# Three softmaxes whose rows are turned by a product with a diagonal of inverse sums

## The chip, the cores and the metric

The kernel runs on one core of a Trainium2 chip. A core has a matrix engine (TensorE, PE in the profile, with its weight loads listed apart as PEld), three engines for elementwise work (VectorE or DVE, ScalarE or ACT, GpSimd or POOL) and a sync engine (SP) that issues most transfers. Matrix products land in PSUM, eight banks of 128 partitions by 512 float32 values; the other data live in SBUF or, between stages, in memory. The metric is the device time of one execution in microseconds (us).

## The reference: three blocks, each with attention in it

The program is a chain of three transformer-like blocks over 1024 tokens of 1024 features. Block one mixes gating, a state space branch and a cross attention of 4 heads to 256 memory rows. Block two mixes a gated recurrence, 6 heads of stick-breaking attention and 6 heads of forgetting attention, followed by a feed-forward part. Block three has a convolution branch and latent attention of 8 heads, again followed by a feed-forward part. Three of these attentions are softmaxes:

```python
# cross attention, block one
p = jax.nn.softmax(s * (XA_HEAD_DIM ** -0.5), axis=-1)
o = jnp.einsum('bhlm,bmhd->blhd', p, vh)
# forgetting attention, block two: causal, with a bias from cumulative gates
p = jax.nn.softmax(jnp.where(mask, s, NEG_BIG), axis=-1)
o = jnp.einsum('bhqs,bhsd->bhqd', p, v)
```

Latent attention in block three is a softmax over all 1024 keys. Stick-breaking attention is no softmax: its weights come from a running product of sigmoids, and nothing is divided by a sum.

## The kernel before

Activations lie with features on partitions and tokens along the free dimension, in two halves of 512 tokens. To keep float32 accuracy, most products are done in three parts (`mm3`, L286 to L290): each operand is split into a high and a low part of a type called F32R, and three of the four cross products are added in PSUM.

An attention head works as follows. For each block of 128 query tokens the scores go to a PSUM tile `sp` with tokens on partitions and keys along the row. DVE takes the negated maximum of each row (`mx`), ACT computes the exponentials into the SBUF tile `pp` and at the same time adds up each row into `den`, one number per partition. That is L995 to L998 in cross attention, L1672 to L1674 in `causal_head`, and L2176 to L2180 in `mla_head`.

Then the rows have to be turned, because the product with the values needs keys on partitions. For each slice of 128 keys, four 128x128 blocks of `pp`, one per block of query tokens, are transposed by PE into one bank `ps_t` (L1003, L1686, L2189; there are two such banks). `av` (L1011) copies the bank as a high part with ACT (L1020) and takes the low part with DVE (L1021); two products with the values add up in the bank `ps_o` (L1025, L1026). In stick-breaking heads, which share `causal_head`, L1023 and L1024 take the place of L1020 and L1021.

At the end of each half, `av_out` (L896) adds the two halves of partitions of `ps_o` into `yo` (L901, L902). For a softmax it also divides: it takes the reciprocal of each `den` (L906), spreads it to 128 columns and transposes it on PE into a bank `ps_t` (L907), so that the inverse sums lie along the free dimension, and multiplies `yo` by that (L908). The result goes to memory and is read back as input of the output product.

What sets the order of the work: a framework schedules all instructions at build time by their order in the program, their priorities and its own costs, and each engine then works through its list in that order. `staggered` (L1612) mixes two heads: scores of the first half of a head, then the turn and value product of the second half of the head before it, then the scores of the second half, then the turn of the first half. Between them, `pump` (L438) fetches pieces of side work, the output product of rows that are ready, at a lower priority.

Buffers matter as well. In `causal_head` the tiles `pp` of the first half (512 columns) have 5 buffers and those of the second half (1024 columns) have 6; one half of a head needs 4. In `mla_head` there are 8 for two halves. `L1647` fills two rows of a query tile on POOL at the start of each forgetting head.

Of the kernel before, what the change touches and what calls it, by code (L numbers as in the profile page):

```python
# [10 lines left out]
F32 = mybir.dt.float32  # L11
# [3 lines left out]
ALU = mybir.AluOpType  # L15
# [4 lines left out]
P = 128  # L20
# [3 lines left out]
HF = 512  # L24
# [151 lines left out]
class Kern:  # L176
# [716 lines left out]
                nc.sync.dma_start(ybd[64 * gb:64 * gb + 64, t, :].rearrange("(g c) k -> c g k", c=16), yo[t * 16:(t + 1) * 16])  # L893


    def av_out(self, po, odd, out, dens=None):  # L896

        nc = self.nc
        a, b = (64, 0) if odd else (0, 64)
        r = slice(a, a + 64)  # L900
        nc.scalar.copy(out[r, :], po[b:b + 64, :])  # L901
        nc.vector.tensor_tensor(out[r, :], po[r, :], out[r, :], op=ALU.add)  # L902
        if dens:
            tp = self.pt("t")
            for j, den in enumerate(dens):
                nc.vector.reciprocal(den, den)  # L906
                nc.tensor.transpose(tp[:, j * P:(j + 1) * P], den.to_broadcast([P, P]), self.ident)  # L907
            nc.vector.tensor_tensor(out[r, :], out[r, :], tp[r, :], op=ALU.mult)  # L908

    def v_stack(self, ps, vst, scale=1.0):  # L910

# [63 lines left out]
    def cross(self, pc, p1, xs, y, kst, vst):  # L975
        nc, d = self.nc, self.d
        for i in range(2):
            def ev(hf, ps):
                hi = pc.tile([P, HF], F32R, tag="qh", bufs=1, name="qh")
                lo = pc.tile([P, HF], F32R, tag="ql", bufs=1, name="ql")  # L980
                nc.scalar.mul(hi, ps, 0.125)
                nc.vector.scalar_tensor_tensor(lo, ps, 0.125, hi.bitcast(F32), op0=ALU.mult, op1=ALU.subtract)
                qs = [pc.tile([P, HF], F32R, tag="qs", bufs=2, name="qs") for _ in range(2)]
                self.stack_pair(hi, lo, qs)
                for o in range(2):
                    h = 2 * i + o
                    pp = pc.tile([P, 4, 256], F32, tag="pp", bufs=2, name="pp")
                    sp = self.pt("s", (P, 4, 256))
                    for tt in range(4):
                        for j in range(2):  # L990
                            nc.tensor.matmul(sp[:, tt, :], qs[o][:, tt * P:(tt + 1) * P], kst[h][:, j, :], start=j == 0, stop=j == 1)
                    if o == 0:
                        self.pump()
                    mx = self.small("mx", (P, 4))
                    nc.vector.tensor_reduce(mx, sp, axis=AX, op=ALU.max, negate=True)  # L995
                    den = self.small("den", (P, 4))
                    for tt in range(4):
                        nc.scalar.activation(pp[:, tt, :], sp[:, tt, :], AF.Exp, bias=mx[:, tt:tt + 1], accum_out=den[:, tt:tt + 1])  # L998
                    po = self.pt("o")
                    for m in range(2):  # L1000
                        tp = self.pt("t")
                        for tt in range(4):
                            nc.tensor.transpose(tp[:, tt * P:(tt + 1) * P], pp[:, tt, m * P:(m + 1) * P], self.ident)  # L1003
                        self.av(pc, tp, vst[m][:, h, :], po, m == 0, m == 1)
                    yo = p1.tile([P, HF], F32, tag="tmp", bufs=3, name="yo")
                    self.av_out(po, o, yo, [den[:, tt:tt + 1] for tt in range(4)])
                    r = slice(64 * o, 64 * o + 64)
                    nc.vector.scalar_tensor_tensor(y[6 + i][hf][r], yo[r], 0.5, y[6 + i][hf][r], op0=ALU.mult, op1=ALU.mult)
            self.gemm(d["w_in"][16 + i], xs, ev)
# [613 lines left out]
    def causal_head(self, pl, pa, src, h, yd, row, fox):  # L1623
        nc = self.nc
        qs = []
        for hf in range(2):
            q = self.h("qs", "S", F32R)
            nc.sync.dma_start(q.bitcast(F32), src["q"][h, :, hf * HF:(hf + 1) * HF])
            qs.append(q)
        kk, qa = [], qs  # L1630
        for j in range(2):
            k = pl.tile([P, T], F32R, tag="k", bufs=4, name="k")
            f = k.bitcast(F32)
            nc.sync.dma_start(f[0:64], src["k"][h, j])
            if fox is None or j == 0:
                nc.sync.dma_start(f[64:128], src["k"][h, j])
            else:
                nc.sync.dma_start(f[64:66], fox[h])
            kk.append(k)
        rows = P  # L1640
        if fox is not None:

            qa, rows = [], 66
            for hf in range(2):
                q = pl.tile([P, HF], F32R, tag="q2", bufs=2, name="q2")
                nc.sync.dma_start(q.bitcast(F32)[0:64], src["q"][h, 0:64, hf * HF:(hf + 1) * HF])
                nc.gpsimd.memset(q.bitcast(F32)[64:66], -1.0)  # L1647
                qa.append(q)
        odd = h % 2
        vst = pl.tile([P, KT, P], F32R, tag="vst", bufs=2, name="vst")  # L1650
        nc.sync.dma_start(vst.bitcast(F32), src["v"][:, :, h, :])
        parts = []
        for hf in range(2):
            pps, dens = [], []
            parts.append((pps, dens))
            for j in range(4 * hf, 4 * hf + 4):
                w = (j + 1) * P
                sp = self.pt("s", (P, T))
                for c0 in range(0, w, HF):
                    c = slice(c0, min(w, c0 + HF))  # L1660
                    t = slice((j % 4) * P, (j % 4 + 1) * P)
                    for i, (q, r) in enumerate(((qs[hf], P), (qa[hf], rows))):
                        nc.tensor.matmul(sp[:, c], q[:r, t], kk[i][:r, c], start=i == 0, stop=i == 1)
                        if i == 0 and c0 + HF >= w:
                            nc.tensor.matmul(sp[:, w - P:w], self.idb, self.strict if fox is None else self.cau, start=False, stop=False)
                pp = pa.tile([P, HF * (hf + 1)], F32, tag=f"pp{hf}", bufs=5 + hf, name="pp")
                if fox is None:
                    self.stick(sp, pp, w)
                else:
                    mx = self.small("fmx", (P, 1), bufs=12)  # L1670
                    den = self.small("fden", (P, 1), bufs=12)
                    nc.vector.tensor_reduce(mx, sp[:, :w], axis=AX, op=ALU.max, negate=True)  # L1672
                    self.last = nc.scalar.activation(pp[:, :w], sp[:, :w], AF.Exp, bias=mx, accum_out=den)
                    dens.append(den)  # L1674
                pps.append(pp)
                if j % 4 == 3:
                    self.pump()
            yield
        for hf, (pps, dens) in enumerate(parts):
            po = self.pt("o")  # L1680
            ns = 4 * hf + 4
            for s in range(ns):
                j0 = max(0, s - 4 * hf)
                tp = self.pt("t")
                for j in range(j0, 4):
                    nc.tensor.transpose(tp[:, j * P:(j + 1) * P], pps[j][:, s * P:(s + 1) * P], self.ident)  # L1686
                self.av(pa, tp, vst[:, s, :], po, s == 0, s == ns - 1, j0 * P, 1.0 if fox is None else None)
            yo = pa.tile([P, HF], F32, tag="yo", bufs=1, name="yo")
            self.av_out(po, odd, yo, dens)
            nc.sync.dma_start(yd[row + 64 * h:row + 64 * h + 64, hf * HF:(hf + 1) * HF], yo[64 * odd:64 * odd + 64])  # L1690
            yield

# [454 lines left out]
    def mla_head(self, pa, h, qd, kd, krd, vd, yd):  # L2147
        nc = self.nc
        odd = h % 2
# [15 lines left out]
        for hf in range(2):  # L2165
            pps, dens = [], []
            parts.append((pps, dens))
            for j in range(4):
                sp = self.pt("s", (P, T))
                t = slice(j * P, (j + 1) * P)  # L2170
# [6 lines left out]
                pp = pa.tile([P, T], F32, tag="pp", bufs=8, name="pp")  # L2177
                nc.scalar.activation(pp, sp, AF.Exp, bias=mx, accum_out=den)
                pps.append(pp)
                dens.append(den)  # L2180
                if j==3:
                    self.pump()
            yield
        for hf, (pps, dens) in enumerate(parts):
            po = self.pt("o")
            for s in range(KT):
                tp = self.pt("t")
                for j in range(4):
                    nc.tensor.transpose(tp[:, j * P:(j + 1) * P], pps[j][:, s * P:(s + 1) * P], self.ident)  # L2189
                self.av(pa, tp, vst[:, s, :], po, s == 0, s == KT - 1)  # L2190
            yo = pa.tile([P, HF], F32, tag="yo", bufs=1, name="yo")
            self.av_out(po, odd, yo, dens)
            nc.sync.dma_start(yd[512 + 64 * h:512 + 64 * h + 64, hf * HF:(hf + 1) * HF], yo[64 * odd:64 * odd + 64])
            yield

# [38 lines left out]
```

## Time and profile before

| | us |
|---|---|
| median of 3 runs | 3093.59 |
| lowest and highest | 3091.27, 3094.7 |
| the profiled execution | 3100.47 |
| its span | 3098.7 |
| PE busy in it | 3015.7 |
| DVE busy | 2298.5 |
| ACT busy | 1404.8 |
| POOL busy | 195.6 |

A row of the profile names the line, the engine and the operation, then output and inputs, then shape and count; after the bar come the busy time in us, the mean duration of one in ns, and the idle time of the engine just before such instructions with what ended it. `cn` is the tile of constants, in which the identity matrix lies. A row of the waits reads: who waited for whom, total us, times, longest. A row of a stretch gives from and to, then its length, then for each engine the busy time and the number of instructions, at last the granted clock of PE, the share of the DMA engines and GB/s. Matmul durations overlap, since a matmul starts before the end of the one ahead of it.

### The profile page before, as it was taken

What the parts mean: (1) busy time and instruction counts of PE and PEld (TensorE: products, weight loads), DVE (VectorE), ACT (ScalarE), POOL (GpSimd) and SP (SyncE); (2) the same over time, 40 slices, a digit from 0 to 9 for tenths busy, and PEclk for the clock granted to TensorE, in tenths of its full rate; (3) what the DMA queues carried; (4) which work ended last, traced back from release to release, by engine and by line L of the source; (5) the groups of instructions that cost most, each with busy time, mean ns of one, the idle gap of its engine ahead of it and who ended that gap; (6) DMA issues with size and microseconds to landing.
All of it is one profiled execution on the core that took longest, in us unless ns stands there. A gap on an engine that the chain in (4) does not pass through costs nothing.

```text
span 3098.7 us, 39672 instructions
## 1 busy us (share of the span) xinstructions
PE 3015.7 (97%) x14472; PEld 2452.9 (79%) x14472; DVE 2298.5 (74%) x3624; ACT 1404.8 (45%) x2215; POOL 195.6 (6%) x266
## 2 busy tenths in 40 slices
PE   8999999999989999999999999999999999999998
PEld 6787878777767777888888888877777888888877
DVE  7757784858589877777867646577779988888766
ACT  3254363424256664444434433255545544454453
POOL 0010012212100000000000022000000000000000
PEclk9999999999999999999999999999999999999999
DMA  4242433332474433444653346642132333365333
GB/s 150 64 119 62 129 126 112 86 85 70 139 195 137 120 126 138 150 150 170 246 199 110 129 114 188 189 145 67 45 121 85 106 102 105 107 222 172 106 99 102
DMA packets 210749, 394.01 MB, mean 127 GB/s; under 512 B 31637, under 2 KB 71957, under 8 KB 210426
## 3 DMA queue, kind: packets, MB, share of 16 engines
q1 hardware_dynamic: 210554, 391.47, 40.1%
q8 instruction: 114, 1.87, 0.2%
q14 instruction: 81, 0.66, 0.1%
HBM read 272.78 MB, written 114.87 MB: 125 GB/s over the span
## 4 chain that ended last, share of the span: by engine, by line
PE 47%; DVE 2%; DMA 2%; ACT 1%; issue 1%; SPq 0%; POOL 0%; POOLq 0%; DVEq 0%; ACTq 0%
PE ps_G L289 9%; PE ps_G L290 9%; PE ps_G L288 9%; PE ps_g L289 2%; PE ps_g L288 2%; PE ps_g L290 2%; PE ps_t L2189 2%; PE ps_o L1025 1%; PE ps_t L288 1%; PE ps_t L290 1%; PE ps_t L289 1%; PE ps_o L1026 1%; PE ps_s L288 1%; PE ps_s L289 1%; PE ps_s L290 1%
## 5 line engine op out<-in xcount | busy, mean ns | idle before, releaser
L288 PE MATMUL ps_G<-xsh,wh 128*128 128x512 f32 (+1 forms) x1024 | 398.8, 389 | 8.0 <-ACT xsh L469 6.1
L289 PE MATMUL ps_G<-xsl,wh 128*128 128x512 f32 (+1 forms) x1024 | 398.4, 389 | 1.5 <-DVE xsl L474 1.5
L290 PE MATMUL ps_G<-xsh,wl 128*128 128x512 f32 (+1 forms) x1024 | 397.9, 389 | 1.1 <-DVE wl L309 0.6
L282 ACT CAST wh<-wr 128x1024 fp32r<-128x1024 f32 (+1 forms) x151 | 154.3, 1024 | 272.9 <-PE ps_G L289 74.9
L283 DVE TENSOR_TENSOR wl<-wr,wh 128x1024 fp32r<-128x1024 f32 (+1 forms) x151 | 181.9, 1208 | 82.9 <-ACT wh L282 81.9
L288 PEld LDWEIGHTS ps_G<-xsh,wh 128*128 128x128 f32 x1024 | 193.6, 189 | 47.2 <-ACT xsh L469 6.1
L289 PEld LDWEIGHTS ps_G<-xsl,wh 128*128 128x128 f32 x1024 | 193.2, 189 | 40.6 <-DVE xsl L474 3.1
L290 PEld LDWEIGHTS ps_G<-xsh,wl 128*128 128x128 f32 x1024 | 193.2, 189 | 40.2 <-DVE wl L309 1.5
L288 PE MATMUL ps_g<-xsh,wh 128*128 128x512 f32 (+1 forms) x472 | 186.8, 396 | 0.3 <-ACT xsh L469 0.3
L289 PE MATMUL ps_g<-xsl,wh 128*128 128x512 f32 (+1 forms) x472 | 186.0, 394 | 0.4 <-DVE xsl L474 0.2
L290 PE MATMUL ps_g<-xsh,wl 128*128 128x512 f32 (+1 forms) x472 | 185.2, 392 | 0.0
L288 PE MATMUL ps_G<-xe,wh 128*128 128x512 f32 x440 | 173.2, 394 | 3.9 <-ACT xe L327 3.2
L289 PE MATMUL ps_G<-xe,wh 128*128 128x512 f32 x440 | 172.8, 393 | 0.2 <-DVE xe L328 0.2
L290 PE MATMUL ps_G<-xe,wl 128*128 128x512 f32 x440 | 172.5, 392 | 0.0
L1021 DVE TENSOR_TENSOR ptl<-ps_t,pth 128x512 fp32r<-128x512 f32 x216 | 132.4, 641 | 52.5 <-ACT pth L1020 51.1
L288 PE MATMUL ps_G<-wh,wph 128*128 128x512 f32 x432 | 168.2, 389 | 0.7 <-ACT fz L1325 0.7
L290 PE MATMUL ps_G<-wh,wpl 128*128 128x512 f32 x432 | 168.1, 389 | 0.0
L289 PE MATMUL ps_G<-wl,wph 128*128 128x512 f32 x432 | 168.1, 389 | 0.0
L1020 ACT CAST pth<-ps_t 128x512 fp32r<-128x512 f32 x216 | 112.1, 552 | 109.5 <-PE ps_t L2189 73.8
L308 ACT CAST wh<-hr 128x1024 fp32r<-128x1024 f32 (+1 forms) x98 | 99.8, 1018 | 64.2 <-PE ps_G L290 19.8
L308 ACT CAST wh<-ss 128x1024 fp32r<-128x1024 f32 x68 | 71.4, 1049 | 126.3 <-PE ps_G L289 83.7
L309 DVE TENSOR_TENSOR wl<-hr,wh 128x1024 fp32r<-128x1024 f32 (+1 forms) x98 | 115.6, 1183 | 16.9 <-ACT wh L308 16.9
(611 smaller groups left out, 7550.5 us busy)
## 6 DMA issues: line engine op xcount, KB each, us to landing
wr<-in_w_in_dram SPq DMA_DIRECT2D x65, 512.0 KB, 3.4
wr<-in_w_up_dram SPq DMA_DIRECT2D x44, 512.0 KB, 4.0
wr<-in_w_ff_dram SPq DMA_DIRECT2D x33, 512.0 KB, 4.0
hr<-hT SPq DMA_DIRECT2D x32, 512.0 KB, 3.6
r<-in_w_ff_dram SPq DMA_DIRECT2D x28, 512.0 KB, 4.8
h<-fa SPq DMA_DIRECT2D x48, 256.0 KB, 2.3
hT<-ft SPq DMA_DIRECT2D x48, 256.0 KB, 2.1
hr<-h SPq DMA_DIRECT2D x24, 512.0 KB, 3.8
```

What stands on the lines that cost most here:

```text
L282: nc.scalar.copy(hi[:, :n], raw[:, :n])
L283: nc.vector.tensor_tensor(lo[:, :n], raw[:, :n], hi[:, :n].bitcast(F32), op=ALU.subtract)
L288: mm(out, sh, mh, start=start, stop=False, **kw)
L289: mm(out, sh, ml, start=False, stop=False, **kw)
L290: mm(out, sl, mh, start=False, stop=stop, **kw)
L308: self.nc.scalar.copy(hi, src)
L309: self.nc.vector.tensor_tensor(lo, src, hi.bitcast(F32), op=ALU.subtract)
L1020: nc.scalar.copy(hi[:, c0:], tp[:, c0:])
L1021: nc.vector.tensor_tensor(lo[:, c0:], tp[:, c0:], hi[:, c0:].bitcast(F32), op=ALU.subtract)
L1025: nc.tensor.matmul(po[:, c0:], vs, hi[:, c0:], start=start, stop=False)
L1026: nc.tensor.matmul(po[:, c0:], vs, lo[:, c0:], start=False, stop=stop)
L2189: nc.tensor.transpose(tp[:, j * P:(j + 1) * P], pps[j][:, s * P:(s + 1) * P], self.ident)
```

## The change

Two helpers are new. `over` takes the reciprocal of a `den` and has POOL multiply the identity matrix by it, row by row, into a tile `dg`: a diagonal matrix of inverse sums. `turned` puts a block of `pp` into the bank. Without a diagonal it transposes as before. With one it is an ordinary product, `pp` block transposed times diagonal, of two float32 operands. What comes out is the transposed block, each column of which is multiplied by the inverse sum of its query token. So the turned rows are already normalized.

All three softmaxes use it: each gets four diagonals per half when its exponentials are made. The division at the end of `av_out` is gone (L903 to L908). Stick-breaking heads keep their transposes. The diagonals have 8 buffers in cross attention and 12 in the other two. In `causal_head` the buffers of `pp` go from 5 to 4 and from 6 to 5, for stick-breaking heads as well, as they share the code and the pool.

```diff
-    def av_out(self, po, odd, out, dens=None):
+    def av_out(self, po, odd, out):
...
-        if dens:
-            tp = self.pt("t")
-            for j, den in enumerate(dens):
-                nc.vector.reciprocal(den, den)
-                nc.tensor.transpose(tp[:, j * P:(j + 1) * P], den.to_broadcast([P, P]), self.ident)
-            nc.vector.tensor_tensor(out[r, :], out[r, :], tp[r, :], op=ALU.mult)
+
+    def over(self, pool, den, bufs):
+        g = pool.tile([P, P], F32, tag="dg", bufs=bufs, name="dg")
+        self.nc.vector.reciprocal(den, den)
+        self.nc.gpsimd.tensor_scalar(g, self.ident, den, None, op0=ALU.mult)
+        return g
+
+    def turned(self, out, x, by):
+        if by is None:
+            self.nc.tensor.transpose(out, x, self.ident)
+        else:
+            self.nc.tensor.matmul(out, x, by, start=True, stop=True)
...
+                    dg = [self.over(pc, den[:, tt:tt + 1], 8) for tt in range(4)]
...
-                            nc.tensor.transpose(tp[:, tt * P:(tt + 1) * P], pp[:, tt, m * P:(m + 1) * P], self.ident)
+                            self.turned(tp[:, tt * P:(tt + 1) * P], pp[:, tt, m * P:(m + 1) * P], dg[tt])
...
-                    self.av_out(po, o, yo, [den[:, tt:tt + 1] for tt in range(4)])
+                    self.av_out(po, o, yo)
...
-                pp = pa.tile([P, HF * (hf + 1)], F32, tag=f"pp{hf}", bufs=5 + hf, name="pp")
+                pp = pa.tile([P, HF * (hf + 1)], F32, tag=f"pp{hf}", bufs=4 + hf, name="pp")
...
-                    dens.append(den)
+                    dens.append(self.over(pa, den, 12))
...
-                    nc.tensor.transpose(tp[:, j * P:(j + 1) * P], pps[j][:, s * P:(s + 1) * P], self.ident)
+                    self.turned(tp[:, j * P:(j + 1) * P], pps[j][:, s * P:(s + 1) * P], dens[j] if dens else None)
...
-            self.av_out(po, odd, yo, dens)
+            self.av_out(po, odd, yo)
...
-                dens.append(den)
+                dens.append(self.over(pa, den, 12))
...
-                    nc.tensor.transpose(tp[:, j * P:(j + 1) * P], pps[j][:, s * P:(s + 1) * P], self.ident)
+                    self.turned(tp[:, j * P:(j + 1) * P], pps[j][:, s * P:(s + 1) * P], dens[j])
...
-            self.av_out(po, odd, yo, dens)
+            self.av_out(po, odd, yo)
```

## The prediction

> **What bounds the kernel now.** I read the page first (its shares and its chain), then the stages that the change touches, one row each, then the waits, the chain and the order of instructions inside one stage.
>
> ```profile
> span 3098.7 us, 39672 instructions
> PE 3015.7 (97%) x14472; PEld 2452.9 (79%) x14472; DVE 2298.5 (74%) x3624; ACT 1404.8 (45%) x2215; POOL 195.6 (6%) x266
> ```
> ```profile
> core 0: us, PE busy (x) PEld busy (x) DVE busy (x) ACT busy (x) POOL busy (x), PEclk, DMA share, GB/s
> 210.00:277.00 67.00, 66.87 (x355) 52.64 (x354) 46.78 (x94) 36.38 (x100) 6.17 (x4) 1.00 0.20 57
> 848.00:973.00 125.00, 108.53 (x587) 80.16 (x587) 111.38 (x143) 73.64 (x131) 0.00 (x0) 0.96 0.67 183
> 973.00:1112.00 139.00, 135.43 (x770) 103.40 (x769) 113.33 (x227) 90.50 (x204) 5.18 (x10) 1.00 0.35 102
> 2000.00:2280.00 280.00, 278.18 (x1430) 213.97 (x1429) 209.41 (x324) 163.18 (x290) 0.13 (x2) 1.00 0.29 88
> ```
>
> The four stretches are cross attention, the stick-breaking heads, the forgetting heads and latent attention. The first, third and fourth hold the three softmaxes that change. PE is busy for nearly all of them, at a granted clock of 1.00, while DVE is at 70 to 82% and POOL is almost empty. Since matmuls overlap, a busy PE is not yet a full PE. So I price by the distance from start to start.
>
> ```profile
> 2141.75 0.60 PE L2189 MATMUL ps_t<-cn,pp 128*128 128x128 f32 x4
> 2142.10 0.48 PE L290 MATMUL ps_g<-yth,wl 128*128 128x512 f32 x1
> 2142.59 0.50 PE L1025 MATMUL ps_o<-pth,vst 128*128 128x512 f32 x1
> 2142.92 0.40 PE L288 MATMUL ps_g<-yth,wh 128*128 128x512 f32 x1
> ...
> 2144.99 0.39 PE L289 MATMUL ps_s<-k,qs 96*128 96x512 f32 x1
> ...
> 2147.26 0.39 PE L290 MATMUL ps_s<-k,qs 96*128 96x512 f32 x1
> ```
>
> Ten steps of 512 columns from 2144.99 to 2147.26 take 2.27 us: 0.227 us each. Four transposes of 128 columns last 0.60 us, and one alone 0.27 (rows below), so three steps take 0.33: 0.110 us each. In latent attention 512 transposes and the 64 of L907 need 576 x 0.110 = 63.4 us, the other 854 matmuls 854 x 0.227 = 193.9: together 257 of 280 us, 92%. PE is the bound there, with about 23 us of holes. The holes are mostly as at 2142.10: L1025 starts 0.49 after its predecessor instead of 0.23, because ACT's copy of the turned rows (`pth`) was late. The waits say the same, for latent attention and then for the forgetting heads:
>
> ```profile
> PEld ps_o L1025 <- ACT pth L1020: 19.1, 70, 0.5
> ACT pp L2178 <- PE ps_t L2189: 6.8, 5, 1.4
> PEld ps_t L2189 <- DVE yo L908: 0.5, 2, 0.2
> ```
> ```profile
> PEld ps_o L1025 <- ACT pth L1020: 9.6, 32, 0.8
> PEld ps_t L1686 <- DVE yo L908: 1.4, 3, 0.5
> PE ps_o L1025 <- ACT pth L1020: 1.4, 5, 0.4
> POOL q L1647 <- PE ps_s L1663: 223.9, 9, 143.1
> ```
>
> The chain of waits between 2130 and 2165 us is on PE all the time:
>
> ```profile
> by line: PE ps_t L2189 20.4%; PE ps_o L1025 15.8%; PE ps_o L1026 11.4%; PE ps_s L289 10.5%; PE ps_s L290 10.5%; PE ps_s L288 10.5%; PE ps_g L290 6.7%; PE ps_g L289 6.0%; PE ps_g L288 6.0%; PE ps_t L907 2.5%; issue 0.0%
> ```
>
> **The change, part by part.** *The turn itself.* These are the instructions concerned, and one real float32 product of the same shape that the kernel already has, L888:
>
> ```profile
> L2189 PE MATMUL ps_t<-cn,pp 128*128 128x128 f32 x512 | 80.6, 272 | 0.1
> L1686 PE MATMUL ps_t<-cn,pp 128*128 128x128 f32 x432 | 71.4, 274 | 0.2
> L907 PE MATMUL ps_t<-cn,fden 128*128 128x128 f32 x112 | 18.7, 273 | 0.0
> L1003 PE MATMUL ps_t<-cn,pp 128*128 128x128 f32 x64 | 11.9, 277 | 0.0
> L888 PE MATMUL ps_t<-xg,tp 128*128 128x128 f32 x32 | 6.2, 275 | 0.0
> L907 PE MATMUL ps_t<-cn,den 128*128 128x128 f32 x32 | 6.1, 272 | 0.0
> ```
>
> A transpose is one record: 8 heads x 2 halves x 8 slices x 4 blocks = 512 at L2189. L1686 serves twelve heads of 36 blocks; only the six forgetting heads, 216 blocks, change. L1003 changes all 64. L888 stands in a loop of 4 groups inside 4 blocks, 16 products, and leaves 32 records: a product of two plain float32 operands is issued twice. What a pair costs shows where L888 and L889 alternate:
>
> ```profile
> 86.46 0.39 PE L889 MATMUL ps_t<-hs,wb 128*128 128x128 f32 x2
> ...
> 87.80 0.39 PE L889 MATMUL ps_t<-hs,wb 128*128 128x128 f32 x2
> ```
>
> There are five pairs between these two, so six steps in 1.34 us: 0.223 us a product, against 0.110 a transpose. Extra per product: 0.113 us.
>
> The Trainium skill (Perfetto Trace Analysis, section Transposes) says that a logical transpose should use the transpose operation and not a standard matmul, because transposes skip the arithmetic. The trace agrees: 0.110 against 0.223 us.
>
> 792 blocks change (512 + 216 + 64) and the 144 transposes of L907 go. Latent attention: 512 x 0.113 - 64 x 0.110 = +50.8 us. Forgetting heads: 216 x 0.113 - 48 x 0.110 = +19.1. Cross attention: 64 x 0.113 - 32 x 0.110 = +3.7. Together +73.6 us on the engine that bounds these stages.
>
> *What the holes give back.* In a pair of groups, PE issues eight transposes (0.88 us), one filler, and then waits for the copy of the first group. With products the second group alone takes 0.89 us, longer than that copy (0.55 us, below), so the wait could vanish. But the order of the instructions is laid out at build time, and the layout may pull L1025 forward and leave the same hole. Bounds: nothing, or all of 19.1 + 9.6 + 1.4 = 30.1 us. The layout decides, and no row shows how it will fall, so I take half: -15.1.
>
> ```profile
> L1020 ACT CAST pth<-ps_t 128x512 fp32r<-128x512 f32 x216 | 112.1, 552 | 109.5 <-PE ps_t L2189 73.8
> L908 DVE TENSOR_TENSOR yo<-yo,ps_t 64x512 f32<-64x512 f32 x36 | 24.6, 682 | 1.2
> L906 DVE RECIPROCAL fden<-fden 128x1 f32<-128x1 f32 x112 | 15.1, 154 | 19.8 <-ACT pp L2178 16.3 <-ACT pp L1673 3.4
> ```
>
> *The division at the end.* L908 leaves DVE: 24.6 us that lay under PE's work and are worth nothing there. What counts is PE's waits for it (0.5 + 1.4 = -1.9) and the one L908 that ends latent attention, where yo still goes to memory and back before the next product: -0.7.
>
> *The reciprocals* stay 144 in number and already run as soon as a sum is there (L906 above waits for ACT's exponentials). They cost nothing new on DVE, but now stand ahead of the turn.
>
> *The diagonals.* 144 tensor_scalar of 128x128 on POOL. The nearest rows:
>
> ```profile
> L622 POOL TENSOR_SCALAR ws<-ws 128x512 f32<-128x512 f32 x1 | 1.6, 1566 | 13.8 <-DMA bs<-in_gm_bs_dram 13.8
> L1558 POOL COPY vq<-vend 128x1 f32<-128x1 f32 x3 | 1.2, 416 | 2.9 <-DVE vq L1561 2.8
> ```
>
> Bounds 0.42 and 1.57 us; on the line between them a quarter of the columns costs 0.70. That is 101 us of POOL in stages where it does 11 now. The diagonals of a half are asked for only after the previous head's other half has been turned and multiplied, in latent attention 8 x (4 x 0.110 + 2 x 0.227) = 7 us of PE, and that hides them. Without that cover a half would start 0.15 + 0.70 = 0.85 us later, and 36 halves 31 us. Only the first head of a stage has no previous one: +1. Behind a diagonal on POOL's queue stands, in the forgetting heads, the fill of the next head's q2 (L1647), which waits there for scores today (223.9 us above); nobody is later for it.
>
> *One buffer of exponentials less* for the causal heads of both kinds. In latent attention a shortage shows as ACT waiting for the turn (6.8 us, 5 times, at most 1.4). For the causal heads no such wait stands among their waits today. Bounds: 0, or 1.4 us for each of 12 longer halves, 17 us. Nearest is the zero; I take +2.
>
> **Sum.** +73.6 - 15.1 - 1.9 - 0.7 + 1 + 2 = +58.9 us. The profiled execution took 3100.5 us (span 3098.7 and 1.8 around it) and would take 3159.4. It lies 6.9 above the median of 3093.6, so I forecast 3093.6 + 58.9, rounded to 3152, for a median.
>
> **The rivals.** *The holes take all.* PE fills its holes completely in latent attention (23 us) and those at L1025 in the forgetting heads (11 us): 73.6 - 34 - 2.6 = +37, 3131 us. For it: the new group is longer than the copy that PE waits for. Against it: other waits (for scores' banks) have nothing to do with the turn.
>
> *New waits on top.* A diagonal that is late by 0.85 us in each of 28 causal and latent halves (24 us), and the exponentials short of a buffer (17 us): 58.9 - 3 + 41 = +97, 3191 us. For it: order is fixed beforehand and PE takes its work in order, so a late diagonal stops all of PE. Against it: the cover above.
>
> *The second record is free* (the other side). Place: PE between two products. If the second issue of a product hid behind the first, a product would cost the 0.110 us of a transpose, and only the gains would remain: -144 x 0.110 - 1.9 - 0.7 = -18.4, 3075 us. It decides below (15.8 + 2.6) / 792 = 0.023 us extra a product. Against it: the six steps of 0.223 us. For it: only that those products read other data.
>
> *The product costs four turns*, so that the change doesn't cost what its records say: 792 x 0.330 - 15.8 = +246 on PE, less 14.7 for the other terms, +231, 3325 us. For and against it only L888's rows speak: 0.223 is two, not four. The Trainium skill (FP8 and Floating Point Precision, section TensorE Precision Notes) counts four passes through the array for true FP32; in this trace a float32 product has two records, together twice a transpose.
>
> **How the numbers follow.** Forecast case 58% (own range +51 to +74: from three quarters of the holes at L1025 gone to none), holes take all 20%, new waits 12%, free second record 5%, four turns 2%, and 3% for a layout that falls out otherwise, two of them within 0.2%. The range of 3122 to 3186 leaves out the free record, the four turns, the odd layout and the ends of two rivals, about 2 in 10. A change under 0.2%, about 6 us, couldn't be told from none: faster 5%, same 2%, slower 93%.
>
> **What would show it.** The turn's records for the changed heads double (1024, 432 and 128) at a pace of 0.11 us each; L907 and L908 are gone; latent attention grows from 280 us to about 320 and the forgetting heads from 139 to about 153; PE's waits at L1025 shrink but don't vanish; POOL gains about 144 instructions of some 0.7 us; DVE's busy time falls by about 25 us. Stages without softmax keep their lengths. I am wrong if a product's pair takes less than 0.2 us, if PE waits for the diagonals in the middle of a stage, or if the stick-breaking stage, which only loses buffers, grows by more than some us.

## The result, and the profile after

The changed kernel takes 3174.4 us in the median of four runs (3171.5 to 3176.2); the kernel before, beside it, 3094.1 us (3091.3 to 3099.3). These medians lie 80 us apart. The ratio on record, by which this text goes, is 1.0248, with a 95% interval from 1.0235 to 1.0260: slower by about 77 us. Forecast were 3152 us in a range from 3122 to 3186.

The page of the changed kernel, its span and its engines:

```profile
span 3169.7 us, 41358 instructions
PE 3079.7 (97%) x15120; PEld 2541.2 (80%) x15120; DVE 2286.4 (72%) x3588; ACT 1411.3 (45%) x2215; POOL 284.2 (9%) x410
...
PE 80%; DVE 10%; DMA 3%; ACT 3%; issue 2%; POOL 2%; SPq 0%; POOLq 0%; DVEq 0%; ACTq 0%
```

PE has 648 instructions more than before (15120 against 14472), which is 792 extra records for the products less the 144 transposes of the sums. POOL has 144 more, and DVE 36 fewer, the multiplications of L908 in the kernel before. The third line is the page's chain of waits by engine, which is on PE for 80% of the span. DVE's busy time fell by 12 us on the page and not by the 25 that were forecast; the page counts time in which DVE instructions overlap only once, and their durations added up do fall by 24.5.

In the groups of instructions by line, with the records of the changed heads and of the stick-breaking heads, and the diagonals:

```profile
L916 PE MATMUL ps_t<-dg,pp 128*128 128x128 f32 x1584 | 231.5, 277 | 7.0 <-POOL dg L908 6.2
L914 PE MATMUL ps_t<-cn,pp 128*128 128x128 f32 x216 | 34.6, 276 | 0.0
L908 POOL TENSOR_SCALAR dg<-cn,fden 128x128 f32<-128x128 f32 x112 | 70.6, 632 | 525.3 <-DVE fden L907 511.9 <-PE ps_t L916 13.3
L908 POOL TENSOR_SCALAR dg<-cn,den 128x128 f32<-128x128 f32 x32 | 20.0, 640 | 52.7 <-DVE den L907 52.7
```

1584 records for 792 products: two each. Their pace, from the order of instructions on PE inside latent attention:

```profile
2182.40 1.50 PE L916 MATMUL ps_t<-dg,pp 128*128 128x128 f32 x12
2183.68 0.50 PE L1034 MATMUL ps_o<-pth,vst 128*128 128x512 f32 x1
2184.02 0.40 PE L290 MATMUL ps_s<-k,qs 96*128 96x512 f32 x1
```

Twelve records last 1.50 us and one 0.275, so a step is 1.225 / 11 = 0.111 us, as long as that of a transpose.

Where the time went by stage can be read from the first and the last start of the exponentials of each attention (the two times behind the durations). Before:

```profile
L998 ACT ACTIVATE pp<-ps_s,mx x32: 462/474/483, 210.3 to 272.3; 128x256 f32<-128x256 f32 x32
L1699 ACT ACTIVATE pp<-ps_s x48: 269/648/1028, 848.3 to 965.4; 128x128 f32<-128x128 f32 x6, 128x256 f32<-128x256 f32 x6, 128x384 f32<-128x384 f32 x6, 128x512 f32<-128x512 f32 x6
L1673 ACT ACTIVATE pp<-ps_s,fmx x48: 367/744/1119, 973.4 to 1090.7; 128x128 f32<-128x128 f32 x6, 128x256 f32<-128x256 f32 x6, 128x384 f32<-128x384 f32 x6, 128x512 f32<-128x512 f32 x6
L2178 ACT ACTIVATE pp<-ps_s,fmx x64: 1109/1120/1139, 2002.2 to 2251.1; 128x1024 f32<-128x1024 f32 x64
```

And after:

```profile
L1006 ACT ACTIVATE pp<-ps_s,mx x32: 462/473/488, 210.5 to 286.7; 128x256 f32<-128x256 f32 x32
L1708 ACT ACTIVATE pp<-ps_s x48: 271/652/1027, 864.7 to 982.6; 128x128 f32<-128x128 f32 x6, 128x256 f32<-128x256 f32 x6, 128x384 f32<-128x384 f32 x6, 128x512 f32<-128x512 f32 x6
L1682 ACT ACTIVATE pp<-ps_s,fmx x48: 367/748/1125, 990.1 to 1119.5; 128x128 f32<-128x128 f32 x6, 128x256 f32<-128x256 f32 x6, 128x384 f32<-128x384 f32 x6, 128x512 f32<-128x512 f32 x6
L2187 ACT ACTIVATE pp<-ps_s,fmx x64: 1108/1115/1130, 2028.2 to 2315.7; 128x1024 f32<-128x1024 f32 x64
```

The end of latent attention is the last addition of `yo`, before and after:

```profile
L902 DVE TENSOR_TENSOR yo<-ps_o,yo x48: 655/689/697, 217.4 to 2277.7; 64x512 f32<-64x512 f32 x48
```
```profile
L902 DVE TENSOR_TENSOR yo<-ps_o,yo x48: 656/689/697, 218.0 to 2342.7; 64x512 f32<-64x512 f32 x48
```

| from the first exponentials of | before, us | after, us | grown | predicted |
|---|---|---|---|---|
| cross to stick-breaking | 638.0 | 654.2 | +16.2 | +3.7 |
| stick-breaking to forgetting | 125.1 | 125.4 | +0.3 | up to +2 |
| forgetting to latent | 1028.8 | 1038.1 | +9.3 | +12.2 |
| latent, to the last addition | 275.5 | 314.5 | +39.0 | +40.7 |
| from there to the end | 821.0 | 827.0 | +6.0 | -0.7 |

With the +0.2 ahead of cross attention that makes 71.0 us, the difference of the two spans. The profiled execution of before (3100.5 us) was slower than the four runs above, and that of after was its fastest, so the spans differ by less than the medians.

Two lines stand out in the waits. In cross attention after (210 to 295 us), PE waits for the diagonals:

```profile
PEld ps_t L916 <- POOL dg L908: 11.9, 19, 1.9
PE ps_t L916 <- POOL dg L908: 5.6, 7, 1.1
```

The two rows must not be added: weight loads (PEld) and products (PE) can stand idle in the same pause, and then each row counts it. One such pause:

```profile
218.82 0.39 PE L290 MATMUL ps_G<-xsh,wl 128*128 128x512 f32 x1
218.90 2.76 POOL L908 TENSOR_SCALAR dg<-cn,den 128x128 f32<-128x128 f32 x4 [3.92 <-DVE den L907]
219.97 0.52 PEld L916 LDWEIGHTS ps_t<-dg,pp 128*128 128x128 f32 x4 [1.19 <-POOL dg L908]
219.98 0.71 PE L916 MATMUL ps_t<-dg,pp 128*128 128x128 f32 x4 [0.77 <-POOL dg L908]
220.00 0.17 DVE L907 RECIPROCAL den<-den 128x1 f32<-128x1 f32 x1 [0.29 <-ACT pp L1006]
```

PE starts 1.16 us after the product before it instead of 0.227, so 0.93 us are lost, where the two rows count 1.19 and 0.77. The last reciprocal of this half ends at 220.17 and the last of its four diagonals at 221.66.

And in latent attention after, the wait of the value product for ACT has fallen from 19.1 us to 2.7, while that of the second value product, of the low part, for DVE has risen from 2.4 to 7.4. The first row is from before, the others from after:

```profile
PEld ps_o L1026 <- DVE ptl L1021: 2.4, 10, 0.4
```
```profile
PEld ps_o L1035 <- DVE ptl L1030: 7.4, 38, 0.2
PEld ps_o L1034 <- ACT pth L1029: 2.7, 8, 0.7
PEld ps_t L916 <- POOL dg L908: 1.3, 2, 0.8
```

### The profile page after: what moved, and what is told of

Same layout as the page of the kernel before. It is cut to its first block, busy times and chain, and to the rows that moved or that the text cites. A ratio compares the mean times of both kernels' runs of the same rounds, so it can differ in the third digit from the quotient of the medians.

```text
span 3169.7 us, 41358 instructions
## 1 busy us (share of the span) xinstructions
PE 3079.7 (97%) x15120; PEld 2541.2 (80%) x15120; DVE 2286.4 (72%) x3588; ACT 1411.3 (45%) x2215; POOL 284.2 (9%) x410
## 4 chain that ended last, share of the span: by engine, by line
PE 80%; DVE 10%; DMA 3%; ACT 3%; issue 2%; POOL 2%; SPq 0%; POOLq 0%; DVEq 0%; ACTq 0%
PE ps_G L288 13%; PE ps_G L290 13%; PE ps_G L289 13%; PE ps_t L916 5%; PE ps_g L288 4%; PE ps_g L289 4%; PE ps_g L290 4%; PE ps_o L1034 2%; PE ps_o L1035 2%; PE ps_t L288 1%; PE ps_t L289 1%; PE ps_t L290 1%; PE ps_o L290 1%; PE ps_o L288 1%; PE ps_o L289 1%
## 5 line engine op out<-in xcount | busy, mean ns | idle before, releaser
L282 ACT CAST wh<-wr 128x1024 fp32r<-128x1024 f32 (+1 forms) x151 | 154.3, 1024 | 272.9 <-PE ps_G L289 71.4
L916 PEld LDWEIGHTS ps_t<-dg,pp 128*128 128x128 f32 x1584 | 224.6, 191 | 29.9 <-POOL dg L908 13.2
L916 PE MATMUL ps_t<-dg,pp 128*128 128x128 f32 x1584 | 231.5, 277 | 7.0 <-POOL dg L908 6.2
```

What stands on the lines that cost most here:

```text
L282: nc.scalar.copy(hi[:, :n], raw[:, :n])
L916: self.nc.tensor.matmul(out, x, by, start=True, stop=True)
```

## The experiments

All ratios are to the kernel before, run beside each of them. For the changed kernel it is 1.0248.

**The parts one by one: products, diagonals, buffers.** First the product without its diagonal: the constant identity stands in its place.

```diff
-        g = pool.tile([P, P], F32, tag="dg", bufs=bufs, name="dg")
-        self.nc.vector.reciprocal(den, den)
-        self.nc.gpsimd.tensor_scalar(g, self.ident, den, None, op0=ALU.mult)
-        return g
+        return self.ident
```

> Left out: the division by the sums. The changed heads are turned by a float32 product with the constant identity; no diagonal and no reciprocal is made. Theory (the doubled passes of PE cost the time, and waits for diagonals only the 17.5 us that PE lost in cross attention): about 3157 us, 63 above before. Rival (PE waiting for diagonals all over, or POOL's work, carries most of the loss): at most 3120 us.

3160.2 us, ratio 1.0207 (1.0187 to 1.0228). Some 13 us of the 77 are gone; about 64 stay with no diagonal in the program. Cross attention to stick-breaking took 643.6 us here, 10.6 less than in the changed kernel.

Then the diagonals without the product:

```diff
-        if by is None:
-            self.nc.tensor.transpose(out, x, self.ident)
-        else:
-            self.nc.tensor.matmul(out, x, by, start=True, stop=True)
+        self.nc.tensor.transpose(out, x, self.ident)
```

> Left out: the division by the sums. The diagonals are still made on POOL, but nobody reads them; the rows are turned by transposes as before, and the division at the end is gone. Theory: PE loses the 144 transposes of sums (15.8 us) and some 2 us of waits and gains nothing, so about 3076 us. Rival (reciprocals and diagonals cost DVE or the exponentials' chain something by themselves): 3094 us or more.

3082.4 us, ratio 0.9956 (0.9942 to 0.9970): 14 us faster than before, where the theory had 18. So 144 diagonals on POOL, the reciprocals and the smaller buffers cost nothing that outweighs the gains when nobody waits for them. Between these two kernels lie 0.0251 of 3094 us, 78 us, for 792 second records: 0.098 us net for each, against the 0.113 of the prediction before the holes. They differ in the diagonals too, which only the second kernel makes; if these cost some of the 4 us that it is short of the theory, a record costs up to 0.104.

The buffers alone, in the kernel before:

```diff
-                pp = pa.tile([P, HF * (hf + 1)], F32, tag=f"pp{hf}", bufs=5 + hf, name="pp")
+                pp = pa.tile([P, HF * (hf + 1)], F32, tag=f"pp{hf}", bufs=4 + hf, name="pp")
```

> The kernel before with one buffer of exponentials less in the causal heads (4 and 5) and nothing else. Theory: no more than 3 us above before (3094 to 3097 us), as the stick-breaking stage kept its length in the changed kernel. Rival (the buffers hold back the next head's exponentials): 3102 us or more.

3100.6 us, ratio 1.0010 (1.0001 to 1.0020): about 3 us, the theory's end and within what can hardly be told from none.

**Cross attention.** The changed kernel with the old code there (old `av_out` kept for it, transposes and division):

```diff
-                    dg = [self.over(pc, den[:, tt:tt + 1], 8) for tt in range(4)]
...
-                            self.turned(tp[:, tt * P:(tt + 1) * P], pp[:, tt, m * P:(m + 1) * P], dg[tt])
+                            nc.tensor.transpose(tp[:, tt * P:(tt + 1) * P], pp[:, tt, m * P:(m + 1) * P], self.ident)
...
-                    self.av_out(po, o, yo)
+                    self.av_out(po, o, yo, [den[:, tt:tt + 1] for tt in range(4)])
```

> The changed kernel, but cross attention transposes and divides at the end as before. Theory (cross attention has no other head under which a diagonal could be made, so its 15.7 us come from there): 12 to 16 us below the changed kernel, 3158 to 3162 us. Rival (the 15.7 us came with another order of the side work): 3170 us or more.

3153.3 us, ratio 1.0176 (1.0156 to 1.0197), 0.0072 or 22 us under the changed kernel: more than expected. The stage itself gave 16.8 (637.4 us to stick-breaking); the other 5 are about what runs of one kernel differ by.

Is it POOL's part that PE waits for there? DVE makes the diagonals of cross attention alone:

```diff
-        self.nc.gpsimd.tensor_scalar(g, self.ident, den, None, op0=ALU.mult)
+        (eng or self.nc.gpsimd).tensor_scalar(g, self.ident, den, None, op0=ALU.mult)
...
-                    dg = [self.over(pc, den[:, tt:tt + 1], 8) for tt in range(4)]
+                    dg = [self.over(pc, den[:, tt:tt + 1], 8, nc.vector) for tt in range(4)]
```

> The changed kernel, with the diagonals of cross attention (only these) made by DVE instead of POOL. Theory (PE waits there for four diagonals of 0.60 us in a row behind POOL's other work): PE's waits for diagonals in cross attention fall from 17.5 to under 8 us and the time by 6 to 14 us, to 3160 to 3168. Rival (the chain of exponential, reciprocal and hand-over is what PE waits for, not POOL's part): 3171 us or more.

3164.4 us, ratio 1.0202 (1.0187 to 1.0217): by the ratios 14 us less than the changed kernel, at the edge of the theory; by the medians it is 10. Cross attention to stick-breaking took 645.5 us, 8.7 less than in the changed kernel, so the stage itself bears out less than the 14. The same waits now, from 205 to 300 us:

```profile
PEld ps_t L916 <- ACT pp L1006: 2.3, 6, 1.0
PE ps_t L916 <- DVE den L907: 0.6, 1, 0.6
```

DVE needs 0.29 us for a diagonal (median), POOL 0.60. In the changed kernel the last diagonal of a half is ready 1.2 to 2.4 us after its last reciprocal, here 0.3 to 0.4. The waits that are left come to 2.9 us at most, so the rival falls: it was mostly POOL's four in a row.

**What in a product costs?** Each block turned by two transposes into the same place:

```diff
-            self.nc.tensor.matmul(out, x, by, start=True, stop=True)
+            self.nc.tensor.transpose(out, x, self.ident)
+            self.nc.tensor.transpose(out, x, self.ident)
```

Here too `over` returns the constant identity.

> Left out: the division by the sums. No diagonals; each block of the changed heads is turned by a transpose, and the same transpose is issued a second time into the same place. Theory (what costs is the second record of 0.11 us, whatever it computes): within 6 us of the product with the identity, so 3154 to 3166 us. Rival (float32 arithmetic or the slower weight load, 192 against 140 ns, adds to it): 3145 us or less.

3181.0 us, ratio 1.0252 (1.0235 to 1.0270). Both expectations missed: it is slower than the product with the identity by 0.0045, 14 us. Since the two kernels also wait differently, the times alone can't say what a record costs. The distances from start to start can. Here seven transposes stand in a row:

```profile
2102.07 0.27 PE L914 MATMUL ps_t<-cn,pp 128*128 128x128 f32 x1
...
2102.72 0.27 PE L914 MATMUL ps_t<-cn,pp 128*128 128x128 f32 x1
```

Six steps take 0.65 us, 0.108 each. Twelve records of the product with the identity:

```profile
2115.13 1.50 PE L913 MATMUL ps_t<-cn,pp 128*128 128x128 f32 x12
```

That is 0.111 a step, as in the changed kernel. Over 1584 records the difference makes some 5 us, not the 15 or more of the rival, which falls: the second record costs, nearly whatever it computes. But the count isn't all. Latent attention takes 326.9 us here and 314.1 with the identity. The waits of the value products in it, first for this kernel:

```profile
PEld ps_o L1032 <- ACT pth L1027: 26.7, 105, 0.9
PEld ps_o L1033 <- DVE ptl L1028: 3.6, 19, 0.3
```

and for the product with the identity:

```profile
PEld ps_o L1032 <- DVE ptl L1027: 7.6, 39, 0.2
PEld ps_o L1031 <- ACT pth L1026: 4.2, 11, 1.5
```

With separate transposes, the wait for ACT is no smaller than before the change (19.1); with products it is nearly gone. PE's records are the same in number, so it is the layout, made at build time, that differs. A likely reason is that it knows a product to be longer than one transpose; that wasn't tested by itself.

**Can the holes be filled without a product?** The two products with the values in `av` get a later place, in the kernel before:

```diff
-        nc.tensor.matmul(po[:, c0:], vs, hi[:, c0:], start=start, stop=False)
-        nc.tensor.matmul(po[:, c0:], vs, lo[:, c0:], start=False, stop=stop)
+        with self.behind(10):
+            nc.tensor.matmul(po[:, c0:], vs, hi[:, c0:], start=start, stop=False)
+            nc.tensor.matmul(po[:, c0:], vs, lo[:, c0:], start=False, stop=stop)
```

> The kernel before, transposes and all; only the two products of each turned group with the values (L1025, L1026) get a place 10 later in the order by which the layout picks instructions. Theory (the holes at L1025 are a matter of layout: other work stood ready, and the changed kernel got back some 16 us of them because its products took longer in the layout): PE's waits at L1025 for ACT in latent attention fall from 19.1 to under 8 us and the time falls by 5 to 20 us, to 3075 to 3090. Rival (there is nothing ready to fill the holes with, only a longer turn covers them): no change, or slower as the value products end later, 3094 us or more.

3089.6 us, ratio 0.9975 (0.9963 to 0.9986). Latent attention shrank from 275.5 to 262.1 us and its wait for ACT to 3.6, but the stick-breaking stage, 125.1 before, took 131.9.

The same with 30:

> As with 10, but 30 later, which is behind the side work (20 later) too. Theory (layout): the waits at L1025 fall at least as far, 3070 to 3090 us. Rival (nothing to fill with): 3094 us or more.

3083.7 us, ratio 0.9952 (0.9940 to 0.9965), 15 us faster than before. Latent attention takes 259.1 us, stick-breaking 125.7; the stretch from the forgetting heads to latent attention is 8.9 us shorter than before, the end behind latent attention 7.9 longer. What PE waits for there now:

```profile
PEld ps_t L2190 <- DVE ptl L1021: 9.1, 41, 0.4
PEld ps_s L288 <- ACT pp L2179: 7.0, 24, 0.7
PEld ps_o L1026 <- ACT pth L1020: 2.9, 13, 0.4
```

L1026 is here the first value product. Work did stand ready for the holes, and the rival (nothing to fill with) falls. The largest wait left is for the pair of banks `ps_t`: a turn waits until DVE has read the bank.

The same edit with 30 in the changed kernel:

> The changed kernel with the value products 30 later in the layout's order. Theory (in latent attention the changed kernel has already filled the holes at L1025, 2.7 us are left of 19.1, so there is little to gain a second time; in cross attention a later value product doesn't bring the diagonals sooner): 3166 to 3176 us. Rival (30 later helps whatever the turn is): 3160 us or less, as it took 14 us off the kernel before.

3169.0 us, ratio 1.0224 (1.0206 to 1.0241). The interval overlaps that of the changed kernel without the edit (1.0235 to 1.0260), so a gain isn't sure, and at 0.0024 it is half of the 0.0048 that the edit gives the kernel before. Latent attention went from 314.5 to 312.2, where the kernel before went from 275.5 to 259.1: the changed kernel had filled those holes already.

**Dividing ahead of the turn without a second record.** In forgetting and latent attention the row itself is scaled in place; cross attention and the transposes stay as before (in `mla_head` alike):

```diff
-                    dens.append(den)
+                    nc.vector.reciprocal(den, den)
+                    nc.gpsimd.tensor_scalar(pp[:, :w], pp[:, :w], den, None, op0=ALU.mult)
```

> Division moved ahead of the turn without a second record: in forgetting and latent attention POOL multiplies each row of exponentials by its inverse sum in place, the rows are turned by transposes, and the division at the end is gone there; cross attention as before. Theory: PE loses 112 transposes (12 us), and the four rows of a half take POOL about 4 x 2.9 = 11.4 us in latent attention, less than the 17.5 us of a half, so 3080 to 3092 us. Rival (rows come too late and PE waits for them): 3100 us or more.

3104.6 us, ratio 1.0016 (1.0006 to 1.0027): between theory and rival, and no gain. POOL's row of 1024, among the groups of instructions, and then PE's waits for scaled rows in latent attention (L2191) and in the forgetting heads (L1687):

```profile
L2181 POOL TENSOR_SCALAR pp<-pp,fden 128x1024 f32<-128x1024 f32 x64 | 184.2, 2893 | 114.3 <-DVE fden L2180 65.1 <-PE ps_t L2191 48.2 <-PE ps_g L290 0.9
```
```profile
PEld ps_t L2191 <- POOL pp L2181: 6.2, 4, 2.6
PE ps_t L2191 <- POOL pp L2181: 4.6, 3, 2.2
PEld ps_t L1687 <- POOL pp L1675: 12.4, 6, 3.1
PE ps_t L1687 <- POOL pp L1675: 10.9, 6, 2.9
```

The two rows of a stage count in part the same pauses. Taken once for each stage, they are 15.5 to 18.6 us of new waits, more than the 12 us that PE saved, and the larger part lies in the forgetting heads.

With `nc.vector` in place of `nc.gpsimd`:

> As the kernel with rows scaled on POOL, but DVE scales them. Theory: DVE has some 70 us free in latent attention and needs at most 64 x 1.2 = 77 us less the 11 us of the divisions; it is about even, 3085 to 3100 us. Rival (DVE becomes the bound of latent attention): 3110 us or more. Rival (DVE scales a row of 1024 in about half its usual 1.2 us, so that it fits): 3088 us or less.

3099.8 us, ratio 0.9994 (0.9984 to 1.0003): no difference. A row of 1024 costs DVE 0.75 us, and PE waits under 1 us for scaled rows; the holes for ACT stay (18.1 us).

Both together, rows scaled by DVE and the value products 30 later:

> Rows scaled on DVE ahead of the turn in forgetting and latent attention, and the value products 30 later. Theory: what the two give adds up, at most the 12 us of 112 transposes saved on PE on top of the kernel with 30 alone, 3060 to 3088 us. Rival (DVE's added work eats it): not below the kernel with 30 alone.

3080.8 us, ratio 0.9939 (0.9925 to 0.9953): faster than both the kernel before and the changed one. Its interval overlaps with that of the later value products alone (0.9940 to 0.9965), so the part of the scaled rows isn't shown.

## Why the prediction was right, and where its terms were off

*The turn itself, +73.6 us.* Right. The records doubled, their pace is 0.111 us, the identity product shows 64 us that no diagonal causes, and the unused diagonals show that the rest of the change alone would have been a gain. The Trainium skill's sentence that was weighed there (Perfetto Trace Analysis, section Transposes: a transpose should be a transpose) holds here at two to one. The rivals of a free second record and of four turns are out: 0.098 us net a record is neither nothing nor three times 0.11. The rival in which the holes take all (3131 us) is out by the time.

*What the holes give back, -15.1 us.* The mechanism was right, and the sum came close. In latent attention the wait of the first value product fell by 16.4 us, not by half of 19.1, but that of the second rose by 5.0, and such rows of weight loads aren't PE's loss to the full. The stage itself tells more. It grew by 39.0 us, though 15 products of the next stage, 3.4 us, left it (see below), so for the same work it grew by 42.4. Of +50.8 - 0.5 the holes thus gave back 50.8 - 0.5 - 42.4 = 7.9 us, where 9.6 were forecast. In the forgetting heads the waits of 9.6 and 1.4 fell to the first of these rows, while the second was 1.4 before (990 to 1140 us, after):

```profile
PEld ps_o L1034 <- ACT pth L1029: 2.1, 9, 0.5
PEld ps_o L1035 <- DVE ptl L1030: 4.0, 20, 0.5
```

The stretch from there to latent attention grew by 9.3 us: 19.1 - 1.4 - 9.3 = 8.4 given back, where 5.5 were forecast. It holds the feed-forward part as well, so this figure is less sure. Together that is 16.3 us against 15.1. The half was a choice between two bounds and not worked out, so that it came this close is in part luck.

*The diagonals, +1 us.* This step failed, in one place. The prediction said that the diagonals of a half are asked for only after another half has been turned, and that only the first head of a stage has no cover. That is so where `staggered` mixes heads: outside cross attention PE's weight loads waited 1.3 us for diagonals. Cross attention isn't written that way: each of its eight halves is scored, turned and finished in one go. There PE waited for diagonals in seven of the eight halves, and the stage grew by 16.2 us instead of 3.7. Without any diagonal it was 10.6 us shorter, with DVE making them 8.7. Some 10.6 of the 12.5 us too many are thus the diagonals' own, 1.3 us a half, where the rival with new waits had 0.85 for one reciprocal and one diagonal: four diagonals stand in a row on POOL, 4 x 0.60 = 2.4 us. By one of the prediction's own signs, PE waiting for the diagonals in the middle of a stage, it was wrong here.

*The buffers, +2 us.* Right: 3 us when done alone, 0.3 in the stick-breaking stage of the changed kernel.

*The division at the end.* -1.9 us for PE's waits was right as far as the waits show (none for L908 is left). The -0.7 behind latent attention didn't show: from the last addition to the end the kernel took 6.0 us more. A part of it is work that only moved. PE did these products of the next stage before that addition, and after the change one of them:

```profile
L288 PE MATMUL ps_G<-yth,wh 128*128 128x512 f32 x6 | 2.4, 408 | 0.0
L290 PE MATMUL ps_G<-yth,wl 128*128 128x512 f32 x5 | 2.1, 427 | 0.0
L289 PE MATMUL ps_G<-ytl,wh 128*128 128x512 f32 x5 | 2.0, 397 | 0.0
```

15 x 0.227 = 3.4 us. The other 2.6 us, plus the 0.7, are open. They need not come from the new way to divide: the two kernels with later value products, which keep the old division, have two and one of these products ahead of that addition, and their ends are 6.7 and 7.9 us longer than before.

*The sum* came out 18 us too low by the ratio, 22 by the medians. Between the two profiled executions the growth was 71.0 against 58.9: cross attention makes +12.5 of the difference, the end +6.7, all other terms together -7.1. The rest lies in the choice of the executions. The result is outside the forecast case's own range (+51 to +74) and about as near to the rival with new waits (3191 us) as to the forecast. That rival's waits did come, but not in the causal and latent halves for which it was priced: they came in cross attention, for which neither of the two had a price beyond the +1. The stated range was wide enough to hold this.

## What to carry to other kernels

Count the records that an operation leaves, not its calls: a product of two plain float32 operands took two steps of 0.111 us where a transpose took one, so a multiplication that looks free inside a turn is paid on PE. A cover that one loop gives (another head's work) must be looked for in every place where a helper is called; the one place without it cost about 10 us. Before work is added to fill or remove a wait of PE, try the order of the instructions: a later place for the product that waits gave 15 us without any other edit.

## What wasn't expected of the hardware

POOL needs 0.60 us for 128x128 float32 and 2.89 for 128x1024 in a tensor_scalar, DVE 0.29 and 0.75 for the same two: DVE is about four times as fast on the long row, but only twice on the short one. Loading the weights for a product took longer in the trace than for a transpose (192 against 140 ns in the median), and still the steps from start to start were nearly equal, 0.111 and 0.110 us.
